# Two 32-column pieces in place of one 64-column piece, for the experts with 96 rows

## The chip, the cores and the metric

The kernel runs on one core of one Trainium2 chip. The metric is the device time of a run in microseconds (us), the median of three runs. One further execution was recorded by the hardware profiler; its rows are what the argument rests on. Engines are named as in the profile: PE is the matrix engine (TensorE), PEld its weight loads, DVE, ACT, POOL and SP the vector, scalar, GpSimd and sync engines; SPq is SP's queue, which issues the transfers.

## The reference

A transformer of three layers on 256 tokens and 256 context tokens, in fp32. Each layer has a mixer and then a mixture of experts. The change is in the first layer's mixture, where all 512 tokens pass through 16 experts of 1024 hidden features; every token goes to two of them. Per expert, with `xblk` the tokens that chose it:

```python
def expert_block(args):
    xblk, e = args
    hid = jax.nn.silu(xblk @ w_gate[e]) * (xblk @ w_up[e])
    return hid @ w_down[e]
```

Each of the three matrices of an expert is 1024 x 1024 fp32, 4.19 MB, so an expert has 12.58 MB of weights. The second layer has the same kind of experts on 256 tokens, the third layer 32 smaller ones.

## The kernel before

**Experts and places.** The experts of the first layer run one after another in 16 places, 0 to 15. A place has a fixed number of rows (tokens), from the table `PLAN`: 96 in places 0, 2, 4, 6, 8, 9, 11, 12 and 14 (nine of them), 32 in place 3, and 64 in the other six. In the second layer every place has 64 rows.

**How an expert is tiled.** The tokens are the stationary operand (loaded into the array), the weights stream through as the moving operand, 512 columns at a time. The contraction (1024) is cut into eight steps k of 128. With 64 rows only half of the array's 128 columns are taken, so two products stand side by side: columns 0 to 63 of the array take one half of a weight's 1024 columns, 64 to 127 the other (line 1595, tiles `gu0` for gate and `gu1` for up). Rows 65 to 96 of a 96-row expert are a part of their own: four products stand side by side, 32 columns of the array each, two for gate and two for up (line 1599, tile `gu2`). The function is `expert_wide`; `x64` and `x32` are the two parts, and either can be missing.

The hidden features are then formed on ACT and DVE and transposed by PE (line 1610, lines 1605 to 1612 in all). The last matrix is used in the same two shapes: line 1627 for the 64-row part (tile `py`, 512 moving columns), line 1631 for the 32-row part (tile `py2`, 256 moving columns). At the end `put` writes the weighted results, and `scatter` (line 1563) adds them to the tokens; `gather` (lines 1486 to 1503) collects the tokens of experts that come later. Pieces of gather and scatter are handed to PE between an expert's steps by `s.work()`. They take the whole array, 128 columns.

**An fp32 product on PE.** In the trace each fp32 product of a line is two records, that is two passes over the moving operand, each with its own weight load: line 1599 has 320 products in the program and 640 MATMUL records.

**What sets the order.** The program is not written as one list: a scheduler sorts each engine's instructions by when their operands are due. So the products of an expert don't stand in the same order in each place. In places 0, 2, 11 and 12 they stand as written, for each k gate, up and then the four of the 32-row part. In places 4, 6, 8, 9 and 14 they are sorted by the page of weights that they read, two steps of k at a time.

**Weights.** A page is 1 MB and holds two steps of k of one matrix; an expert has eight pages for gate and up and four for down. In this layer there are 12 pages (four, six and two in three pools), used in turn by `wpage`, so the next expert's page is written into the page that has the same part in the present one, once PE is done with it. SP issues these transfers in order, lines 1579 and 1622.

Of the kernel before, what the change touches and what calls it, by code (L numbers as in the profile page):

```python
# [20 lines left out]
P = 128  # L21
# [26 lines left out]
# rows for the experts of the first layer, in the order in which they run  # L48
PLAN = (96, 64, 96, 32) + (96, 64, 96, 64) + (96, 96, 64, 96) + (96, 64, 96, 64)
# and of the last one; the first experts there have fixed places  # L50
# [8 lines left out]
def _consts():  # L59
# [4 lines left out]
    # rotation: out[m] = sum_p R[p, m] x[p]  # L64
# [33 lines left out]
    # the places of the experts by rank, the larger ones first  # L98
# [15 lines left out]
def apx(t, off, dims):  # L114
    """A view of a tile's free space: `dims` are [stride, count] in elements."""
    a = t.ap
    return AP(t.tensor, t.offset + off, [list(a[0])] + [list(d) for d in dims])


class Halves:  # L120
    """Tiles as one, split in the second axis."""
# [9 lines left out]
class Tokens:  # L131
    """Tiles [128, 2, D] as one [128, 4, D]."""
# [11 lines left out]
class Columns:  # L144
    """The same room as [128, 8, 512]: features x tokens."""
# [13 lines left out]
class K:  # L159
# [24 lines left out]
    def page(self, src, q=None):  # L184
        """Weights [128, 8, n] of DRAM on one or two pages."""
        n = src.shape[2]
        m = 8 if n <= 256 else 4
        ws = []
        for i in range(0, KT, m):
            w = self.t(self.pg, [P, m, n], "pg")  # L190
            (q or self.nc.sync).dma_start(out=w, in_=src[:, i:i + m, :])
            ws.append(w)
        return Halves(ws)

    # ---------------------------------------------------------------- set-up
    def setup(self, ctx, pages):
# [8 lines left out]
        # the tokens, those of the context apart: they are done with early  # L205
# [10 lines left out]
    def vectors(self, ps, vr):  # L216
        """Packed vectors as columns; silu of the conditioning vectors as stationary operands."""
# [15 lines left out]
    # ---------------------------------------------------------------- adaptive modulation  # L233
    def ada_chunk(self, ps, which, j, parts):
        """512 columns of silu(c) @ w: rows 32 g and 32 g + 1 hold the sums over the k groups."""
# [18 lines left out]
    def ada(self, ps, parts, which, vecs):  # L254
        """Vectors of the modulation as columns: ac[:, vector, k, who]."""
# [16 lines left out]
    def gain(self, which, v, gcol):  # L272
        """(1 + scale) * gain in place."""
# [4 lines left out]
    def as_row(self, ps, tag, which, v, who, row):  # L278
        """A vector of the modulation as a row for every token: [128, 1024]."""
# [9 lines left out]
    # ---------------------------------------------------------------- norms  # L289
    def rstd(self, src, n, pool):  # L290
        """1 / sqrt(mean(src^2) + eps) of each row."""
# [14 lines left out]
    def h_transposed(self, ps, pool, hT, tiles, acol, bcol, src=None):  # L306
        """hT[:, k, tokens] = (x * rstd)^T * acol + bcol, as two parts; tiles: (x tile, which vector)."""
# [12 lines left out]
    def transposed(self, ps, pool, hT, g0, who, xn, acol, bcol):  # L320
        """hT[:, k, tokens of tiles g0, g0 + 1] = xn^T * acol + bcol, as two parts."""
# [21 lines left out]
    # ---------------------------------------------------------------- products in three passes  # L343
    def split(self, pool, w, tag, bufs, copy=None):
        """The pages of a weight as two parts, the second on further pages."""
# [15 lines left out]
    def proj_tok(self, ps, hT, t, w, c0, n):  # L361
        """[128 tokens of tile t, n columns] = h @ w[:, c0:c0 + n]"""
# [7 lines left out]
    def proj_feat(self, ps, hT, w, c0, t0, nt):  # L370
        """[128 columns from c0, nt tokens from t0] = (h @ w)^T"""
# [7 lines left out]
    def lower_bounds(self):  # L379
        """lb and 1 - lb as columns [128, dir * 4 + head] of the first layer."""  # L380
# [18 lines left out]
    def head_norm(self, ps, A, o, gate, col, yT, slot):  # L399
        """rms norm over the features of a head [128 tokens, 4 tiles, 128], gate, and yT[:, slot]."""  # L400
# [100 lines left out]
    def rope_t(self, ps, A, src, out):  # L501
        """Axial rotary embedding of 256 tokens on features x tokens, in place in out."""
# [70 lines left out]
    def out_proj(self, ps, A, yT, w, tiles, rows, layer, tmp=None, x0=None):  # L573
        """x += gate * (y @ w), and the router's logits of each tile; w: the two halves of the columns."""
# [12 lines left out]
    def begin_B(self, name):  # L587
        """A pool for what is done with before the mixer's last product."""
# [4 lines left out]
    def end_B(self, st, n, name, h=True):  # L593
        """In its room the normed tokens, as two parts, if asked for, and n pages for the experts' first weights,
        and above them a pool for the last product."""
# [9 lines left out]
    def split_y(self, A, yT, tags):  # L605
        """The mixer's result as two parts."""
# [7 lines left out]
    def router_start(self, ps, A, layer):  # L614
        """The router on x: its weights take the gain, its bias the shift."""
# [33 lines left out]
    def router(self, ps, A, layer, t):  # L649
        """Logits of a tile of tokens, and the tokens' 1 / rms."""  # L650
# [26 lines left out]
    def mixer0(self):  # L677
        tc, nc, I = self.tc, self.nc, self.I
        with ExitStack() as st:
# [29 lines left out]
            # the result takes the room of x, which is read again for the sum  # L709
# [40 lines left out]
    # ---------------------------------------------------------------- second mixer  # L750
# [58 lines left out]
    def swa_block(self, ps, A, q, k, v, b, sink, nsink, swa, yT):  # L809
        """Two heads (of neighbouring key heads) on 128 partitions."""  # L810
# [42 lines left out]
    # ---------------------------------------------------------------- third mixer  # L853
    def early2(self, tmp):
        """What the third mixer needs of the positions and of the decay alone."""
# [39 lines left out]
        # softplus(-lambda) = max(-lambda, 0) + ln(1 + exp(-|lambda|))  # L895
# [15 lines left out]
    def rope_tok(self, A, x, c, s, out):  # L911
        """Rotary embedding of x [128, n, 64], halves apart."""
# [10 lines left out]
    def mixer2(self):  # L923
        tc, nc, I = self.tc, self.nc, self.I
        self.nw2, self.nw4 = 5, 3
        with ExitStack() as st:
# [22 lines left out]
            # the norm of the second block's input and its first layer's in one: x * g * (mean((x g)^2) + eps * ms)^-1/2  # L949
# [190 lines left out]
    def lru(self, ps, A, B, hT, gl, wg, posb, mT):  # L1140
# [13 lines left out]
        for b0 in (0, 2):  # L1154
# [11 lines left out]
            for i in range(2):  # L1166
                # sigmoid(x + b) = (1 + tanh((x + b) / 2)) / 2
# [48 lines left out]
    def ffn_gain(self, which):  # L1216
        """Column of the gain before the experts, and (1 + scale) * gain."""
        self.gain(which, 4, self.vc[:, (V_NF0, V_NF1, V_N2)[which]:][:, 0:8])

    # ---------------------------------------------------------------- experts  # L1220
# [9 lines left out]
    def first_max(self, R, c, weights, tag):  # L1230
        """One-hot of the first largest of the last axis of c [128, nt, n]."""
# [11 lines left out]
    def ranks(self, R, c, m):  # L1243
        """The place of each element of c [128, n, m] in its last axis by falling value, equal ones in order."""
# [12 lines left out]
    def chosen(self, R, rk, goh, E, ng):  # L1257
        """One-hots [128, 2, nt, E] of the first two places rk within the group that goh [128, nt, ng] marks."""
# [41 lines left out]
    def route_softmax(self, R, L, nt, normed):  # L1300
# [8 lines left out]
        def weights():  # L1309
# [9 lines left out]
            # weights p_group * (1, e) / (1 + e) with e = exp(second - first)  # L1319
# [13 lines left out]
    def pad(plan):  # L1333
        """Rows in front of the first expert's, so that the last expert's end a block."""
        return -sum(plan) % P

    def slots(self, ps, R, oh, nt, E, plan):
        """Rows of the experts' buffers for each token's two experts, far off where an expert's cap is passed.
        Also what the rest needs: the row and cap of each expert, counts and places."""
# [16 lines left out]
        if plan == PLAN2:  # L1356
            # experts with more than 32 rows in front, after those whose places are fixed
# [15 lines left out]
        elif len(set(plan)) > 1:  # L1373
            assert plan == PLAN
            # experts by falling count, the first one fixed
# [7 lines left out]
            # the larger buffers for the experts in front  # L1383
# [23 lines left out]
    def pick(self, R, oh, g, tag):  # L1407
        """[128, 2, nt]: the element of g [128, nt, E] that each one-hot marks."""
# [7 lines left out]
    def places(self, s, R, pos, E):  # L1416
        """The expert at each place, as integers."""
# [14 lines left out]
    def beyond(self, R, oh, info, nt, E, plan, ob):  # L1432
        """Rows over the experts' caps, in blocks of ob: each token's rows, the ends of the experts' blocks, their number."""
# [31 lines left out]
    def gather(self, s, G, sl, base, n, xT):  # L1465
        """xT[:, k, 0:n] = the normed tokens of rows base .. base + n of the experts' buffers, features x rows,
        a piece at a time."""
# [499 lines left out]
```

## Time and profile before

| | us |
|---|---|
| median of three runs | 2270.8 |
| lowest, highest | 2268.87, 2275.35 |
| span of the profiled execution | 2265.9 |
| the first layer's experts in it, from the first product of place 0 (481) to the end of place 15 (1106) | 625 |
| PE busy in these | 608.9 |
| the second layer's experts (1420 to 1827) | 407 |

The profiled execution has no time of its own beside its span; the span runs from its first to its last instruction, and the median of the runs is 4.9 us above it. A busy time of PE counts every stretch in which some matmul is under way, also one in which only part of the array works or in which one matmul drains before the next can start. In the timeline's rows, a row is a run of like instructions: its start, its length to the end of the last one, and their count. Since the last one's end lies beyond the point where the next row may start, what a row costs is read from its start to the next row's start.

### The profile page before, as it was taken

How to read it: one execution, taken by the hardware profiler on the slowest of the kernel's cores; microseconds unless marked ns; L12 is line 12 of the kernel's file. 1: busy time of each engine (PE TensorE's matmuls, PEld its weight loads, DVE VectorE, ACT ScalarE, POOL GpSimd, SP SyncE). 2: the span in 40 equal slices, each digit the busy share in tenths (PEclk: the TensorE clock that was granted, in tenths of full speed). 3: DMA queues.
4: the chain of work that ended last, by engine and by line, in shares of the span. 5: the costliest groups of instructions: out<-in, count | busy, mean ns of one | idle time of the engine just before them, and what ended most of it. 6: DMA issues, size and time to landing. Idle time of an engine off the chain costs nothing. (4 is left out here: it accounts for less than half of the span.)

```text
span 2265.9 us, 27806 instructions
## 1 busy us (share of the span) xinstructions
PE 2027.7 (89%) x10931; PEld 987.7 (44%) x10931; DVE 940.5 (42%) x2121; ACT 549.7 (24%) x1010; POOL 246.9 (11%) x203
## 2 busy tenths in 40 slices
PE   6999989979999999999699989998878779879976
PEld 3766666744232322322265464332222245655422
DVE  4537656255432423332445643222111155555513
ACT  4334444132111111111234432010000045421100
POOL 0000000110301101121300000100000011013202
PEclk9999999989999999999899989999999989989988
DMA  8423425338889888889444568999999986779997
GB/s 304 149 75 130 173 93 195 147 138 318 323 324 338 320 301 306 314 315 353 176 167 149 186 260 339 410 409 409 409 409 409 409 284 238 259 258 362 363 369 275
DMA packets 238428, 632.49 MB, mean 279 GB/s; under 512 B 15440, under 2 KB 83024, under 8 KB 234960
## 3 DMA queue, kind: packets, MB, share of 16 engines
q1 hardware_dynamic: 236736, 626.21, 75.0%
q10 hardware_dynamic: 1552, 4.39, 0.5%
q8 instruction: 90, 1.47, 0.3%
q14 instruction: 50, 0.41, 0.1%
HBM read 629.51 MB, written 1.05 MB: 278 GB/s over the span
## 5 line engine op out<-in xcount | busy, mean ns | idle before, releaser
L1595 PE MATMUL gu<-pg,xT 128*64 128x512 f32 x1984 | 475.7, 603 | 26.3 <-DMA pg<-in_moe_w_up_dram 13.9
L1627 PE MATMUL py<-pg,hT 128*64 128x512 f32 x992 | 249.6, 604 | 24.3 <-DVE hT L1612 18.6
L1567 POOL TENSOR_TENSOR xs<-xs,t 128x512 f32<-128x512 f32 x110 | 142.2, 1301 | 1181.5 <-DVE t L1222 1181.4
L1595 PEld LDWEIGHTS gu<-pg,xT 128*64 128x64 f32 x1984 | 125.6, 136 | 313.3 <-issue 243.9
L1546 DVE SCALAR_TENSOR_TENSOR w<-py,swc,w 32x256 fp32r<-32x256 f32 (+3 forms) x142 | 95.5, 673 | 294.5 <-ACT w L1545 291.9
L375 PE MATMUL mm<-hT,wh 128*128 128x512 f32 (+1 forms) x672 | 190.5, 367 | 9.1 <-ACT w L431 5.1
L1545 ACT ACTIVATE w<-py,swc 32x256 fp32r<-32x256 f32 (+3 forms) x142 | 88.2, 621 | 428.0 <-PE py L1627 327.0
L1222 DVE TENSOR_TENSOR hid<-hid,gu 128x512 f32<-128x512 f32 (+2 forms) x52 | 32.8, 631 | 362.2 <-PE gu L1595 297.1
L1222 DVE TENSOR_TENSOR t<-x,w 128x512 f32<-128x512 f32 x156 | 105.8, 689 | 151.1 <-PE x L1563 135.6
L375 PEld LDWEIGHTS mm<-hT,wh 128*128 128x128 f32 x672 | 118.5, 192 | 41.0 <-issue 8.9
L1563 PE MATMUL x<-w,S 128*128 128x512 f32 x312 | 115.8, 450 | 21.2 <-DVE t L1222 9.6
L1658 PE MATMUL gu<-pg,xT 128*32 128x256 f32 (+1 forms) x1024 | 110.6, 436 | 21.8 <-DMA pg<-in_w_up_dram 17.1
L1627 PEld LDWEIGHTS py<-pg,hT 128*64 128x64 f32 x992 | 62.5, 136 | 147.4 <-issue 100.0
L375 PE MATMUL mm<-hT,pg 128*128 128x512 f32 (+1 forms) x336 | 122.5, 366 | 0.6 <-DVE pg L356 0.6
L1605 ACT ACTIVATE hid<-gu 128x512 f32<-128x512 f32 (+1 forms) x41 | 24.4, 595 | 399.8 <-PE gu L1595 373.4
L1495 PE MATMUL x<-oh,h 128*128 128x256 f32 (+2 forms) x704 | 112.2, 293 | 6.3 <-DVE t L1222 2.4
L1495 PEld LDWEIGHTS x<-oh,h 128*128 128x128 f32 x704 | 91.7, 189 | 57.0 <-issue 32.4
L1599 PE MATMUL gu<-pg,xT 128*32 128x512 f32 x640 | 108.1, 604 | 0.0
L1498 ACT ACTIVATE xT<-x,ac 128x256 f32<-128x256 f32 (+2 forms) x88 | 48.3, 549 | 214.8 <-PE x L1495 214.6
L1563 PEld LDWEIGHTS x<-w,S 128*128 128x128 f32 x312 | 50.7, 193 | 108.3 <-issue 31.8
L356 DVE TENSOR_TENSOR pg<-pg,wh 128x1024 fp32r<-128x1024 f32 (+1 forms) x74 | 89.1, 1211 | 20.1 <-ACT wh L355 20.0
L366 PE MATMUL mm<-wh,hT 128*128 128x512 f32 (+2 forms) x320 | 95.1, 377 | 2.1 <-ACT part L247 0.7
(500 smaller groups left out, 2551.6 us busy)
## 6 DMA issues: line engine op xcount, KB each, us to landing
pg<-in_moe_w_gate_dram SPq DMA_DIRECT2D x128, 1024.0 KB, 8.0
pg<-in_moe_w_up_dram SPq DMA_DIRECT2D x128, 1024.0 KB, 8.9
pg<-in_moe_w_down_dram SPq DMA_DIRECT2D x128, 1024.0 KB, 8.6
pg<-in_ada_w_dram SPq DMA_DIRECT2D x48, 1024.0 KB, 6.2
pg<-in_w_gate_dram SPq DMA_DIRECT2D x32, 1024.0 KB, 11.6
pg<-in_w_up_dram SPq DMA_DIRECT2D x32, 1024.0 KB, 11.7
pg<-in_w_down_dram SPq DMA_DIRECT2D x32, 1024.0 KB, 11.2
pg<-in_w_ada_dram SPq DMA_DIRECT2D x24, 1024.0 KB, 6.9
```

What stands on the lines that cost most here:

```text
L356: nc.vector.tensor_tensor(out=u[:, k:k + m], in0=x[:, k:k + m], in1=t[:, k:k + m].bitcast(F32), op=ALU.subtract)
L366: self.nc.tensor.matmul(out=pm, lhsT=hT[i][:, k, t * P:(t + 1) * P], rhs=w[j][:, k, c0:c0 + n], start=(m == 0), stop=(m == len(ops) - 1))
L375: self.nc.tensor.matmul(out=pm, lhsT=w[i][:, k, c0:c0 + P], rhs=hT[j][:, k, t0:t0 + nt], start=(m == 0), stop=(m == len(ops) - 1))
L1222: self.nc.vector.tensor_tensor(out=out, in0=a, in1=b, op=op)
L1495: nc.tensor.matmul(out=px[:, w, :], lhsT=l_, rhs=r_, start=(i == 0), stop=(i == len(ops) - 1))
L1546: nc.vector.scalar_tensor_tensor(out=lo[o:o + m, c0:c0 + w], in0=x, scalar=wc[o:o + m, :], in1=h.bitcast(F32), op0=ALU.mult, op1=ALU.subtract)
L1563: nc.tensor.matmul(out=px, lhsT=S[0:m, t * P:(t + 1) * P], rhs=y[0:m, cols], start=(i == 0), stop=(i == len(parts) - 1))
L1567: (nc.vector if last and h else nc.gpsimd).tensor_tensor(out=o, in0=o, in1=x, op=ALU.add)
L1595: nc.tensor.matmul(out=o[64 * g:64 * g + 64, :], lhsT=x64[0][:, k, x64[1]:x64[1] + 64], rhs=w[:, 512 * g:512 * g + 512], **f)
L1599: nc.tensor.matmul(out=pq[32 * q:32 * q + 32, :], lhsT=x32[0][:, k, x32[1]:x32[1] + 32], rhs=wk[q // 2][:, 512 * (q % 2):512 * (q % 2) + 5 ...
L1627: nc.tensor.matmul(out=py[64 * h:64 * h + 64, :], lhsT=h64[:, b, 64 * g:64 * g + 64], rhs=w[:, kk, 512 * h:512 * h + 512], **f)
L1658: nc.tensor.matmul(out=pg[r * e:r * e + r, 256 * i:256 * i + 256], lhsT=xT[:, k, c0 + r * e:c0 + r * e + r], rhs=ws[e][:, k, :], start=(k ...
```

## The change

In `expert_wide` the width of a piece of the 64-row part becomes a variable, `m64`: 64 as before where there is no 32-row part, and 32 where there is one. A 64-row part then runs as four products side by side instead of two, 32 columns of the array each: two pieces of 32 rows for each half of the weight's columns. The sums are the same, in the same places of PSUM. The new file also has no comments, so its lines are others: 1595 became 1598, 1599 became 1602, 1610 became 1613, 1627 became 1631 and 1631 became 1635.

```diff
+        m64 = 32 if x32 else 64
...
                 for w, o in zip(wk, (pg, pu)) if x64 else ():
-                    for g in range(2):
-                        nc.tensor.matmul(out=o[64 * g:64 * g + 64, :], lhsT=x64[0][:, k, x64[1]:x64[1] + 64],
+                    for q in range(0, P, m64):
+                        g, r = divmod(q, 64)
+                        nc.tensor.matmul(out=o[q:q + m64, :], lhsT=x64[0][:, k, x64[1] + r:x64[1] + r + m64],
                                          rhs=w[:, 512 * g:512 * g + 512], **f)
...
-                for h in range(2) if x64 else ():
-                    nc.tensor.matmul(out=py[64 * h:64 * h + 64, :], lhsT=h64[:, b, 64 * g:64 * g + 64],
+                for q in range(0, P, m64) if x64 else ():
+                    h, r = divmod(q, 64)
+                    nc.tensor.matmul(out=py[q:q + m64, :], lhsT=h64[:, b, 64 * g + r:64 * g + r + m64],
                                      rhs=w[:, kk, 512 * h:512 * h + 512], **f)
```

The order of PE's instructions at two places of the program follows. A row is a line, the operation, what it writes and reads, the stationary columns by the moving columns, and a count of products. SP's order, and so that of the transfers, is the same in both kernels.

PE in place 11, the first two steps of k, as they were (`pg_1320` is a page of gate, `pg_1321` one of up):

```order
L1595 MATMUL gu0_1317_6286<-pg_1320_6289,xT_1123_5309 64x512 x2
L1595 MATMUL gu1_1318_6287<-pg_1321_6290,xT_1123_5309 64x512 x2
L1599 MATMUL gu2_1319_6288<-pg_1320_6289,xT_1123_5309 32x512 x2
L1599 MATMUL gu2_1319_6288<-pg_1321_6290,xT_1123_5309 32x512 x2
L1595 MATMUL gu0_1317_6286<-pg_1320_6289,xT_1123_5309 64x512 x2
L1595 MATMUL gu1_1318_6287<-pg_1321_6290,xT_1123_5309 64x512 x2
L1599 MATMUL gu2_1319_6288<-pg_1320_6289,xT_1123_5309 32x512 x2
L1599 MATMUL gu2_1319_6288<-pg_1321_6290,xT_1123_5309 32x512 x2
```

and as they are now:

```order
L1598 MATMUL gu0_1317_6574<-pg_1320_6577,xT_1123_5501 32x512 x4
L1598 MATMUL gu1_1318_6575<-pg_1321_6578,xT_1123_5501 32x512 x4
L1602 MATMUL gu2_1319_6576<-pg_1320_6577,xT_1123_5501 32x512 x2
L1602 MATMUL gu2_1319_6576<-pg_1321_6578,xT_1123_5501 32x512 x2
L1598 MATMUL gu0_1317_6574<-pg_1320_6577,xT_1123_5501 32x512 x4
L1598 MATMUL gu1_1318_6575<-pg_1321_6578,xT_1123_5501 32x512 x4
L1602 MATMUL gu2_1319_6576<-pg_1320_6577,xT_1123_5501 32x512 x2
L1602 MATMUL gu2_1319_6576<-pg_1321_6578,xT_1123_5501 32x512 x2
```

Nothing changes its turn; the 64-column pairs have become 32-column fours, so the width is 32 throughout where it went between 64 and 32.

PE in place 4, the first two steps of k, as they were (`pg_1006` gate, `pg_1007` up):

```order
L1595 MATMUL gu0_1003_4661<-pg_1006_4664,xT_871_4018 64x512 x2
L1599 MATMUL gu2_1005_4663<-pg_1006_4664,xT_871_4018 32x512 x2
L1595 MATMUL gu0_1003_4661<-pg_1006_4664,xT_871_4018 64x512 x2
L1595 MATMUL gu1_1004_4662<-pg_1007_4665,xT_871_4018 64x512 x2
L1599 MATMUL gu2_1005_4663<-pg_1007_4665,xT_871_4018 32x512 x2
L1595 MATMUL gu1_1004_4662<-pg_1007_4665,xT_871_4018 64x512 x2
L1599 MATMUL gu2_1005_4663<-pg_1006_4664,xT_871_4018 32x512 x2
L1599 MATMUL gu2_1005_4663<-pg_1007_4665,xT_871_4018 32x512 x2
```

and as they are now:

```order
L1598 MATMUL gu0_1003_4757<-pg_1006_4760,xT_871_4066 32x512 x4
L1602 MATMUL gu2_1005_4759<-pg_1006_4760,xT_871_4066 32x512 x2
L1598 MATMUL gu0_1003_4757<-pg_1006_4760,xT_871_4066 32x512 x4
L1598 MATMUL gu1_1004_4758<-pg_1007_4761,xT_871_4066 32x512 x4
L1602 MATMUL gu2_1005_4759<-pg_1007_4761,xT_871_4066 32x512 x2
L1598 MATMUL gu1_1004_4758<-pg_1007_4761,xT_871_4066 32x512 x4
L1602 MATMUL gu2_1005_4759<-pg_1006_4760,xT_871_4066 32x512 x2
L1602 MATMUL gu2_1005_4759<-pg_1007_4761,xT_871_4066 32x512 x2
```

Here too each stands at its old turn. The two products of `gu2` that stand alone take two of the four groups of 32 columns: the gate's the first two, the up's the last two.

## Rows read from the trace of the kernel before

**Rows 1.** Page: the span.

```profile
span 2265.9 us, 27806 instructions
```

**Rows 2.** Windows: stretch, length, busy PE, PEld, DVE, ACT, POOL; clock, DMA, GB/s.

```profile
481.00:1106.00 625.00, 608.91 (x3345) 195.65 (x3343) 224.61 (x429) 93.88 (x165) 93.80 (x72) 1.00 0.85 313
1106.00:1420.00 314.00, 283.35 (x1415) 166.02 (x1416) 159.80 (x417) 111.84 (x219) 11.96 (x12) 0.92 0.58 212
1420.00:1827.00 407.00, 343.93 (x1508) 110.36 (x1506) 79.43 (x138) 31.29 (x49) 36.24 (x28) 1.00 1.03 409
```

**Rows 3.** Waits of PE, 481 to 1106: us in total, times, longest.

```profile
PE py L1627 <- DVE hT L1612: 7.4, 9, 1.2
PE x L1563 <- DVE t L1222: 1.9, 5, 0.4
```

**Rows 4.** Waits of SP's queue, 481 to 1106.

```profile
SPq L1622 <- PE gu L1599: 135.2, 20, 32.4
```

**Rows 5.** Timeline of PE: start, length, operation; places 5 and 11.

```profile
698.69 5.37 PE L1595 MATMUL gu<-pg,xT 128*64 128x512 f32 x24
...
925.74 1.94 PE L1595 MATMUL gu<-pg,xT 128*64 128x512 f32 x8
927.60 1.07 PE L1599 MATMUL gu<-pg,xT 128*32 128x512 f32 x8
928.60 1.94 PE L1595 MATMUL gu<-pg,xT 128*64 128x512 f32 x8
...
953.34 1.08 PE L1627 MATMUL py<-pg,hT 128*64 128x512 f32 x4
954.35 0.64 PE L1631 MATMUL py<-pg,hT 128*32 128x256 f32 x8
954.92 1.08 PE L1627 MATMUL py<-pg,hT 128*64 128x512 f32 x4
```

**Rows 6.** Timeline of PE, place 4: two steps of k.

```profile
645.62 1.08 PE L1595 MATMUL gu<-pg,xT 128*64 128x512 f32 x4
646.62 1.05 PE L1599 MATMUL gu<-pg,xT 128*32 128x512 f32 x4
647.61 1.94 PE L1595 MATMUL gu<-pg,xT 128*64 128x512 f32 x8
649.47 1.05 PE L1599 MATMUL gu<-pg,xT 128*32 128x512 f32 x4
650.46 1.08 PE L1595 MATMUL gu<-pg,xT 128*64 128x512 f32 x4
651.47 1.07 PE L1599 MATMUL gu<-pg,xT 128*32 128x512 f32 x8
652.46 1.08 PE L1595 MATMUL gu<-pg,xT 128*64 128x512 f32 x4
```

**Rows 7.** Timeline of PE and of its weight loads, place 3 (32 rows).

```profile
606.98 2.74 PE L1599 MATMUL gu<-pg,xT 128*32 128x512 f32 x18
609.65 0.50 PE L1563 MATMUL x<-w,S 128*128 128x512 f32 x1
...
607.41 0.13 PEld L1599 LDWEIGHTS gu<-pg,xT 128*32 128x32 f32 x4 [0.30 <-issue]
607.84 0.13 PEld L1599 LDWEIGHTS gu<-pg,xT 128*32 128x32 f32 x4 [0.30 <-issue]
```

**Rows 8.** Groups by line, 481 to 1106: busy, mean ns, idle before.

```profile
L1599 PEld LDWEIGHTS gu<-pg,xT 128*32 128x32 f32 x640 | 16.2, 108 | 79.2 <-issue 78.1 <-ACT w L1545 0.8
```

**Rows 9.** Windows of places 3, 4, 11 and 13, as in rows 2.

```profile
607.00:639.00 32.00, 29.71 (x220) 15.14 (x214) 22.79 (x43) 9.67 (x19) 10.44 (x8) 1.00 1.01 391
639.00:682.00 43.00, 42.22 (x234) 9.08 (x232) 7.23 (x21) 3.84 (x8) 0.00 (x0) 1.00 0.82 299
...
923.00:961.00 38.00, 37.22 (x234) 8.79 (x230) 6.69 (x11) 4.12 (x7) 0.00 (x0) 1.00 0.89 331
...
1005.00:1032.00 27.00, 27.00 (x118) 9.62 (x116) 12.96 (x20) 3.23 (x7) 10.49 (x8) 1.00 1.02 401
```

## The prediction

> **What bounds the kernel now.** I began with the page's span of 2265.9 us [rows 1] and the windows by stage. The change touches only places of the first layer's mixture that have a 32-row part, so its stage is 481 to 1106. There PE is busy 608.91 of 625 us at full granted clock, and the transfers bring 313 GB/s [rows 2]. The waits of PE come next: the largest is 7.4 us in nine waits for the transposed hidden features, the second 1.9 us, and none of them is a wait for a transfer [rows 3]. The transfers' own queue waits for PE to give pages back, 135.2 us in its largest entry [rows 4]. So in this stage PE is what ends last, and what PE saves ends the stage earlier. The second layer's experts, at 409 GB/s [rows 2], are the other kind of stage: they have no 32-row part and their code is as it was.
>
> A busy PE is not yet a full PE, so I read its timeline for what a step costs.
>
> Length of a pass. Eight more records in a run of 64-wide pairs are four more rounds (a round: one pass in all column groups). From x8 with 1.94 us to x24 with 5.37 us are eight rounds in 3.43 us [rows 5]: 0.429 us a round. In the 32-wide run of place 3, 18 records are nine products in four groups: the first group has three products of two passes, so six rounds lie between 606.98 and 609.65, 2.67 us [rows 7], 0.429 each and 0.1 for the end. The two widths have the same round. Below, a unit is two rounds, 0.859 us, in which all groups finish one 512-column product.
>
> Price of a change of width. A block of 64-wide records with x8 starts at 925.74, and the 32-wide one behind it at 927.60: 1.86 us for four rounds (1.72). The 32-wide one with x8 takes to 928.60: 1.00 for two rounds (0.86). In the last product, 1.01 for 0.86 and 0.57 for two rounds of 256 columns, 0.43 [rows 5]. Each block costs 0.14 to 0.15 us over its rounds; I take 0.145. Within one width the outputs go from gate to up and back without such a cost: the x24 run does it.
>
> Half-filled blocks. In place 4, in two steps of k, two blocks are 32-wide with x4, two products in two of the four groups; each takes 0.99 us to the next row, as does the full one with x8 [rows 6]. Two steps take 645.62 to 652.46, 6.84 us: seven units (6.01) and six blocks (0.87). Only six units of work are in them.
>
> **The change, part by part.** It adds 48 products to each 96-row expert (32 in gate and up, 16 in down) and no other work; a unit has the same length, so the work of a column group stays 24 units in gate and up plus 12 in down (8 and 4 halved), 36 an expert.
>
> (1) Widths. From the order of the products I count where the width changes in a place, the whole-array pieces included. Before: 40, 39, 43, 43, 43, 54, 34, 40 and 43 in places 0, 2, 4, 6, 8, 9, 11, 12 and 14, in all 379. After: 16, 13, 4, 5, 5, 18, 5, 12 and 5, in all 83. What remains are the changes to and from gather, scatter and transposes. 296 fewer at 0.145 are 42.9 us; pieces of gather that moved add four in places 1, 3 and 5, 0.6. That is 42.3.
>
> (2) Half-filled blocks. In places 4, 6, 8 and 14 the two products that stood alone between 64-wide blocks now stand between 32-wide ones. A group that they leave free can go on with the next products: the first pair delays groups 0 and 1, the second groups 2 and 3, and after six units all groups are level. One unit less in two steps, four an expert: 4 x 4 x 0.859 = 13.7 us. In place 9 pieces of scatter stand between the two pairs and keep seven units; there (1) alone counts. In place 4 the whole check reads: 41 units (35.2) and 43 blocks (6.2) make 41.4, and the window has 43 [rows 9], so 1.6 are the transposes and the wait for them. After: 37 units (31.8) and 4 blocks (0.6), with the same rest 34.
>
> No row shows two column groups of different tiles at different products. Bounds: if a group waits until all are free, (2) gives 0; if it doesn't, 13.7. In the 32-wide run of place 3 the ninth product starts in group 0 as its turn comes, with no block between k steps [rows 7]; it is the nearest row, and I take 13.7. For (1) the bounds are 0.145 and, if a 32-wide stream that goes between tiles kept some cost, 0; the x24 run, which goes between tiles and keeps none, is nearest.
>
> (3) What may come back. The 0.8 us waits for the transposed features stay, nine of them. The last 32-row block covered the DVE step ahead of the transposes; it becomes 0.14 shorter, nine times, 1.3 us if nothing else covers. Groups that are half a product apart at an expert's end cost up to 0.4 in five places, and scatter behind place 5's kind of start keeps its 1.9 us of waits. I take 2 us.
>
> (4) Transfers. A page is asked for when the expert before gives the same page back [rows 4], a whole expert ahead. After, a 96-row expert of the dense kind takes about 34 us, and 12.58 MB in 34 us is 370 GB/s; places 3 and 13 were served at 391 and 401 [rows 9]. So they stay hidden, with a margin of 6 to 8%. If the cover went, an expert at 331 GB/s, what place 11 has now [rows 9], would take 38 us.
>
> (5) Weight loads. Four of 108 ns instead of two a round [rows 8]. In place 3 four loads begin together, end in 0.13 us and recur every 0.43 us [rows 7], under the passes. Cost 0. If each round paid its 0.13, 9 x 72 rounds would cost 84 us.
>
> Beside this, the Trainium skill, page "TensorE: Matmul & The Clock Gate", section "Part 3: Packing small matmuls — row/col tiling", says that weight loads run under matmuls in flight only where the row group differs. All products here use all 128 rows, so by that rule no load would be hidden, and the sum would be the 84 us loss of the last sentence set against the gain. The trace does not agree: the loads of rows 7 come 0.43 us apart, the length of a bare round.
>
> Sum: 42.3 + 13.7 - 2 = 54 us. On the profiled span that is 2265.9 - 54 = 2212; the median of the runs is 4.9 above the span, so 2270.8 - 54 = 2217 us. The later stages I let move as a whole: the mixer that follows draws 212 GB/s, far under the 409 of the mixture behind it [rows 2], so an earlier start finds the transfers free, and the pages of that mixture are given back by the mixer, which starts earlier by as much.
>
> **The rivals.**
> Main case, both terms: 2217, own range 2210 to 2224. Chance 0.70.
> Groups wait for each other: (2) falls, 42.3 - 2 = 40, 2231. For it: no row shows mixed tiles. Against: place 3's odd runs. 0.13.
> Transfers end last: places 4, 6, 8, 11 and 14 stop at 38 us instead of 34 (place 11: 33), 21 us given back, 33 us gain, 2238. For it: the margin is thin, and the stage's mean must rise from 313 to 343 GB/s (195.6 MB in 571 us). Against: 391 to 409 in rows 2 and 9. 0.06.
> The block's cost isn't the width's, but stands wherever the 32-row part alternates with the other: (1) falls, 13.7 - 2 = 12, 2259. Against: it appears at every change between 64, 32 and the whole array, and nowhere else. 0.03.
> Slower: the loads of a long 32-wide stream are not hidden. Place 3's runs are short; a stream of 24 units an expert could use up what was loaded ahead. At 0.13 a round the net is 84 - 54 = 30, so 2301; it decides from 54 / 648 rounds = 0.083 us a round. Against: six rounds in a row show nothing. 0.03.
> The change does not take effect in time: transfers capped at the stage's present mean of 313 GB/s, PE waiting as long as it saves, 2271. Against: the queue waits for PE, not the reverse [rows 4]. 0.03.
> The last 0.02 I leave to what I do not see, faster or not.
>
> **How the numbers follow.** About 0.3% (7 us) tells a change from none here. Faster by more: 0.70 + 0.13 + 0.06 + 0.03 and half of the rest, 0.93. Within: 0.03 and a little, 0.04. Slower: 0.03. The range takes in the main case with its own uncertainty and the two next ones with theirs: 2207 to 2238. It leaves out about 0.11.
>
> **What would show it.** In the timeline after, a 96-row expert has one unbroken 32-wide run in gate and up where no piece of gather or scatter stands; its rounds recur every 0.43 us. Step (1): place 11 takes about 33 us for 38. Step (2): two steps of k in place 4 take 5.2 us for 6.84; 6.0 would be the first rival. Step (3): PE's waits in the stage near 16 us, as now. Step (4): no wait of PE for a page of gate, up or down there; the stage's rate near 343 GB/s. Step (5): loads 0.13 us long in fours. The stage should end near 1052 for 1106, and what follows should keep its length. The prediction is wrong if rounds grow beyond 0.43, if PE waits for pages, or if the stages behind give time back.

## The result, and the profile after

| | before | after |
|---|---|---|
| median, us (four runs each) | 2270.1 | 2213.6 |
| lowest, highest | 2268.9, 2275.4 | 2210.0, 2221.6 |
| ratio of the times, 95% interval | 1 | 0.9747 (0.9731 to 0.9763) |
| span of the profiled execution | 2265.9 | 2219.7 |
| first layer's experts, in it | 624.99 | 566.68 |

The change saves 56.5 us on the medians, where 54 was forecast (2217 us against 2213.6). The interval of the ratio allows 53.8 to 61.1 us.

The two profiles differ by 46 us of span only, so the stages have to be set against each other one by one. First the windows from the first product of place 0 to the end of place 15, the mixer behind, and the rest of the program. Of the kernel before (columns as in [rows 2]):

```profile
481.19:1106.18 624.99, 608.73 (x3344) 195.56 (x3343) 224.44 (x430) 94.01 (x165) 93.80 (x72) 1.00 0.85 313
1106.18:1362.53 256.35, 225.88 (x1142) 143.13 (x1142) 140.69 (x354) 100.82 (x200) 11.96 (x12) 0.91 0.51 179
1362.53:2265.90 903.37, 769.25 (x4170) 343.62 (x4169) 312.09 (x706) 165.63 (x319) 113.42 (x91) 0.96 0.94 352
```

and of the changed one, with a short stretch near its end:

```profile
488.12:1054.80 566.68, 551.39 (x4208) 224.32 (x4207) 224.95 (x430) 94.19 (x165) 94.02 (x72) 1.00 0.91 345
1054.80:1311.19 256.39, 225.16 (x1142) 142.51 (x1142) 140.60 (x354) 100.80 (x200) 11.95 (x12) 0.91 0.51 179
1311.19:2219.70 908.51, 772.41 (x4170) 346.08 (x4169) 312.02 (x706) 165.75 (x319) 114.40 (x91) 0.96 0.94 350
...
1893.00:1906.00 13.00, 12.75 (x58) 7.53 (x62) 6.28 (x14) 5.11 (x9) 0.76 (x2) 0.50 0.31 104
```

The stage of the change is 58.3 us shorter; PE is busy 57.3 us less in it and idle 1.0 us less (16.3 before, 15.3 after). PE's records are 864 more, and its weight loads are busy 29 us more, all under other work. The transfers' rate rises from 313 to 345 GB/s. The mixer behind it has its old length to 0.04 us. The 12 us by which the spans fall short of the 58 are 7 us ahead of the stage (it starts at 488 for 481, and the change touches nothing ahead of it) and 5 us behind it. The last row shows 13 us at the lower of TensorE's two levels (a granted clock of 0.50, 1.2 GHz); the same place of the program before, 51.3 us later, had the full one:

```profile
1944.30:1957.30 13.00, 12.62 (x93) 8.53 (x94) 10.44 (x20) 9.98 (x17) 0.56 (x1) 1.00 0.68 237
```

Such a stretch comes and goes by the run: of the ten profiles of this study, from the first expert of the second layer to PE's last record, five take 894.4 to 895.3 us (the kernel before among them), one 897.0 and four 899.6 to 900.0 (the changed kernel among them). Exactly those four have 13.7 us at a granted clock of 0.50 at this place. In the 6.9 us ahead of it PE was busy for 6.90 us; at the same place of the kernel before, where the clock stayed at its full level, for 6.70. So these rows do not show why it fell. The changed kernel's profiled run is the longest of its four, 2221.6 us. For that reason the stage is compared below, not the span.

Place 11 in PE's timeline after, which answers to the middle of [rows 5]:

```profile
888.86 1.92 PE L1598 MATMUL gu<-pg,xT 128*32 128x512 f32 x16
890.60 1.04 PE L1602 MATMUL gu<-pg,xT 128*32 128x512 f32 x8
891.46 1.90 PE L1598 MATMUL gu<-pg,xT 128*32 128x512 f32 x16
893.18 1.04 PE L1602 MATMUL gu<-pg,xT 128*32 128x512 f32 x8
...
908.63 1.04 PE L1602 MATMUL gu<-pg,xT 128*32 128x512 f32 x8
909.69 0.66 PE L1613 MATMUL tp<-cst,hid 128*128 128x128 f32 x4
```

From 890.60 to 893.18 is one step of k, three units: 2.58 us, 0.86 each. Nothing is left of the 0.14 to 0.15 us that each block cost. Its weight loads, in the same stretch (the last bracket is what ended the engine's idle time):

```profile
893.18 0.13 PEld L1602 LDWEIGHTS gu<-pg,xT 128*32 128x32 f32 x4 [0.30 <-issue]
893.61 0.13 PEld L1598 LDWEIGHTS gu<-pg,xT 128*32 128x32 f32 x4 [0.30 <-issue]
894.04 0.13 PEld L1598 LDWEIGHTS gu<-pg,xT 128*32 128x32 f32 x4 [0.30 <-issue]
```

Four loads in 0.13 us every 0.43 us, as in [rows 7]: hidden in the long run too. The sentence of the Trainium skill on loads that was set against the change ("TensorE: Matmul & The Clock Gate", "Part 3: Packing small matmuls — row/col tiling") does not hold here as it stands: every product uses all 128 rows, and the loads still lie under the passes. The same section also lets a load go ahead into a background weight buffer; whether that is what happens here, no row shows.

Place 4 after, two steps of k, which answers to [rows 6]:

```profile
637.80 1.04 PE L1598 MATMUL gu<-pg,xT 128*32 128x512 f32 x8
638.66 0.60 PE L1602 MATMUL gu<-pg,xT 128*32 128x512 f32 x2
638.67 0.62 PE L1598 MATMUL gu<-pg,xT 128*32 128x512 f32 x2
639.09 0.60 PE L1602 MATMUL gu<-pg,xT 128*32 128x512 f32 x2
639.12 1.85 PE L1598 MATMUL gu<-pg,xT 128*32 128x512 f32 x12
640.41 0.60 PE L1602 MATMUL gu<-pg,xT 128*32 128x512 f32 x2
...
642.09 1.06 PE L1602 MATMUL gu<-pg,xT 128*32 128x512 f32 x8
642.95 1.06 PE L1598 MATMUL gu<-pg,xT 128*32 128x512 f32 x8
```

The rows of line 1602 and of line 1598 start 0.01 to 0.04 us apart: two column groups run the 32-row part while the other two already run the next product. Two steps go from 637.80 to 642.95, 5.15 us for 6.84, which is six bare units (5.15).

PE's waits in the stage after, which answer to [rows 3] (us in total, times, longest):

```profile
PE py L1631 <- DVE hT L1615: 6.2, 8, 0.8
PE x L1563 <- DVE t L1222: 2.8, 5, 0.9
PE x L1563 <- ACT w L1545: 1.8, 3, 0.8
PE tp L1613 <- DVE hid L1222: 1.7, 2, 0.9
```

No wait for a transfer is among them. The windows of places 4, 11 and 9 after, in this order; the first two answer to [rows 9]:

```profile
637.80:671.87 34.07, 33.28 (x333) 12.46 (x325) 7.43 (x21) 3.37 (x7) 0.00 (x0) 1.00 0.94 359
888.86:922.00 33.14, 32.34 (x325) 11.58 (x327) 6.66 (x11) 3.91 (x6) 0.00 (x0) 1.00 0.96 364
807.31:850.93 43.62, 43.53 (x357) 14.51 (x349) 16.71 (x27) 6.08 (x11) 10.66 (x8) 1.00 0.82 307
```

and of place 9 before:

```profile
835.96:885.33 49.37, 48.00 (x250) 11.30 (x249) 16.39 (x27) 5.43 (x11) 10.57 (x8) 1.00 0.69 249
```

Place 4 takes 34 us and place 11 33 us, as forecast; place 9 is 5.75 us shorter. The window of place 9 begins 0.8 us before the last products of place 8 are done, since its first products go into a column group that is already free; places 8 and 9 together went from 92.86 to 76.77 us.

### The profile page after: what moved, and what is told of

It is laid out like the page before. It is cut to its first block, busy times and chain, and to the rows that moved or that the text cites. A ratio compares the mean times of both kernels' runs of the same rounds, so it can differ in the third digit from the quotient of the medians.

```text
span 2219.7 us, 29536 instructions
## 1 busy us (share of the span) xinstructions
PE 1978.9 (89%) x11795; PEld 1023.2 (46%) x11795; DVE 940.9 (42%) x2121; ACT 549.9 (25%) x1010; POOL 248.2 (11%) x203
## 5 line engine op out<-in xcount | busy, mean ns | idle before, releaser
L1598 PE MATMUL gu<-pg,xT 128*64 128x512 f32 (+1 forms) x2560 | 489.0, 598 | 27.1 <-DMA pg<-in_moe_w_up_dram 14.6
L1631 PE MATMUL py<-pg,hT 128*64 128x512 f32 (+1 forms) x1280 | 258.5, 597 | 23.6 <-DVE hT L1615 17.4
L1598 PEld LDWEIGHTS gu<-pg,xT 128*64 128x64 f32 (+1 forms) x2560 | 132.5, 124 | 297.9 <-issue 227.7
L1631 PEld LDWEIGHTS py<-pg,hT 128*64 128x64 f32 (+1 forms) x1280 | 77.0, 124 | 137.4 <-issue 76.2
L1563 PE MATMUL x<-w,S 128*128 128x512 f32 x312 | 112.9, 442 | 22.8 <-DVE t L1222 11.5
```

Of the source, the lines that this page charges most:

```text
L1563: nc.tensor.matmul(out=px, lhsT=S[0:m, t * P:(t + 1) * P], rhs=y[0:m, cols], start=(i == 0), stop=(i == len(parts) - 1))
L1598: nc.tensor.matmul(out=o[q:q + m64, :], lhsT=x64[0][:, k, x64[1] + r:x64[1] + r + m64], rhs=w[:, 512 * g:512 * g + 512], **f)
L1631: nc.tensor.matmul(out=py[q:q + m64, :], lhsT=h64[:, b, 64 * g + r:64 * g + r + m64], rhs=w[:, kk, 512 * h:512 * h + 512], **f)
```

## The experiments

The theory is the prediction's: a price for each change of the array's width, and a unit saved for each two half-filled blocks. Its rivals: all of the gain is the width's, or it belongs to the turn between the two parts of an expert, or a 32-wide product is cheaper in itself. Blocks and units below are counted from the order of the products, from place 0 to the end of place 15, all kernels alike: 491 blocks and 514 units before, 199 and 498 after. Each stage length, and each busy time of PE in it, is from one profile. The runs were made in three groups, each with runs of the kernel before beside it (medians 2270.1, 2271.7 and 2272.8 us), and each ratio is to those.

| kernel | blocks, units | median, us | ratio to before, 95% interval | stage, us | PE busy in it |
|---|---|---|---|---|---|
| before | 491, 514 | 2270.1 to 2272.8 | 1 | 624.99 | 608.73 |
| after | 199, 498 | 2213.6 | 0.9747 (0.9731 to 0.9763) | 566.68 | 551.39 |
| gate_up_alone | 330, 498 | 2232.9 | 0.9830 (0.9813 to 0.9846) | 587.60 | 572.95 |
| down_alone | 356, 514 | 2250.9 | 0.9902 (0.9885 to 0.9918) | 602.36 | 587.38 |
| mixed_64 | 274, 498 | 2225.6 | 0.9793 (0.9777 to 0.9809) | 577.53 | 562.91 |
| all_32 | 191, 499 | 2214.0 | 0.9747 (0.9730 to 0.9763) | 565.21 | 550.94 |
| pairs | 177, 499 | 2214.2 | 0.9751 (0.9734 to 0.9768) | 566.29 | 549.84 |
| split_copy | 201, 496 | 2217.0 | 0.9754 (0.9741 to 0.9768) | 567.23 | 553.25 |
| split_pairs | 179, 497 | 2213.4 | 0.9741 (0.9726 to 0.9756) | 564.77 | 550.33 |
| little_32 | not counted | 2158.3 (one run) | none | 506.33 | 472.00 |

**Half of the change: gate and up.** Against the changed kernel:

```diff
-                for q in range(0, P, m64) if x64 else ():
+                for q in range(0, P, 64) if x64 else ():
...
-                    nc.tensor.matmul(out=py[q:q + m64, :], lhsT=h64[:, b, 64 * g + r:64 * g + r + m64],
+                    nc.tensor.matmul(out=py[q:q + 64, :], lhsT=h64[:, b, 64 * g + r:64 * g + r + 64],
```

> The 64-row part of the 96-row experts runs 32 wide in gate and up, 64 wide in down. From the order: 330 blocks of one width from place 0 to the end of place 15 (491 before, 199 after the change), and 498 units of work (514 before, 498 after), so the half-filled blocks of places 4, 6, 8 and 14 are gone as in the changed kernel. Theory (a price of 0.145 us for each block, and a unit of 0.859 us saved for each half-filled pair of blocks): 161 blocks fewer than before are 23.3 us, 16 units 13.7, together 37: 2270 - 37 = 2233 us; against the changed kernel (2214) +19. Place 4 takes 37 units, 21 blocks and the rest of 1.6 us: 36.4 us (42.8 before, 34.1 after). Rival, all of the gain of 56.5 is in the changes of width, 0.19 us each, and none in the half-filled blocks: 161 x 0.19 = 31 us, 2239, place 4 at 42.8 - 22 x 0.19 = 38.6. Rival, a 32-wide product costs less in itself: two thirds of the products that changed are here, 38 us, 2232.

Measured: 2232.9 us, and place 4 takes 36.26 us. Both are the theory's (2233, 36.4); the rival without the half-filled blocks wanted 2239 and 38.6. The rival of a cheaper 32-wide product wanted 2232 (and by the same reckoning 2251 for the other half, below), which these times can't tell from the theory; it is decided by the two runs on the 64-row experts that follow.

**The other half: down.** The same edit in the loop of gate and up:

```diff
-                    for q in range(0, P, m64):
+                    for q in range(0, P, 64):
...
-                        nc.tensor.matmul(out=o[q:q + m64, :], lhsT=x64[0][:, k, x64[1] + r:x64[1] + r + m64],
+                        nc.tensor.matmul(out=o[q:q + 64, :], lhsT=x64[0][:, k, x64[1] + r:x64[1] + r + 64],
```

> The other half of the change: the 64-row part of the 96-row experts runs 32 wide in down, 64 wide in gate and up. 356 blocks and 514 units: changes of width go, half-filled blocks stay. Theory: 135 blocks fewer than before at 0.145 us are 19.6 us, 2270 - 19.6 = 2250 us; place 4 takes 41 units, 27 blocks and 1.6 us: 40.7 us. Rival, all in the changes of width at 0.19 us: 25.6 us, 2244, place 4 at 39.8. Rival, the cost of the block is not the width's: no gain, 2270.

Measured: 2250.9 us, place 4 at 40.64 us (theory 2250 and 40.7; with all of the gain in the changes, at 0.19 us each, 2244 and 39.8). Its timeline in place 4 has the half-filled blocks still:

```profile
645.50 1.08 PE L1598 MATMUL gu<-pg,xT 128*64 128x512 f32 x4
646.51 1.05 PE L1602 MATMUL gu<-pg,xT 128*32 128x512 f32 x4
647.49 1.94 PE L1598 MATMUL gu<-pg,xT 128*64 128x512 f32 x8
649.36 1.05 PE L1602 MATMUL gu<-pg,xT 128*32 128x512 f32 x4
...
651.35 1.06 PE L1602 MATMUL gu<-pg,xT 128*32 128x512 f32 x8
652.35 1.08 PE L1598 MATMUL gu<-pg,xT 128*64 128x512 f32 x4
```

645.50 to 652.35 is 6.85 us for the two steps, the 6.84 of [rows 6]; the 32-wide blocks with x4 take 0.98 us. So it is the width of gate and up that fills them. The two halves save 37.4 and 22.6 us of the stage, together 60.0 where the whole saves 58.3.

**Changes of width put back elsewhere.** In the 64-row experts every second step of k runs 32 wide; the same is done in down.

```diff
-                    for q in range(0, P, m64):
+                    mw = 32 if s.layer == 0 and kk else m64
+                    for q in range(0, P, mw):
...
-                        nc.tensor.matmul(out=o[q:q + m64, :], lhsT=x64[0][:, k, x64[1] + r:x64[1] + r + m64],
+                        nc.tensor.matmul(out=o[q:q + mw, :], lhsT=x64[0][:, k, x64[1] + r:x64[1] + r + mw],
```

> The changed kernel, and in the six experts of the first layer that have 64 rows and no 32-row part (places 1, 5, 7, 10, 13, 15) every second step of k runs 32 wide, in gate, up and down: same work, more changes of width, and nothing else. 274 blocks for 199 of the changed kernel, units the same. Theory: 75 more changes at 0.145 us cost 10.9 us, 2214 + 11 = 2225; the places grow by 8, 16, 17, 12, 10 and 17 blocks (less one taken away each in places 11 and 13's neighbours), so place 7 from 36.0 to about 38.5 us. Rival, the block's cost is not the width's but stands where a 64-row and a 32-row part alternate: 0, 2214. Rival, 32-wide products cost less in themselves: 144 of them against 432 in the change, a third of 56 us, so 19 us faster, 2195.

Measured: 2225.6 us; the stage is 10.85 us longer than the changed kernel's, 0.145 us for each of the 75 changes (11.5 us by PE's busy time, 0.154). Of these, 0.8 us are in place 14, where no width differs from the changed kernel (34.91 us for 34.09); without it the price is 0.134, or 0.143 by the busy time. At 0.19 us a change, the price that would put the whole gain into the widths, it would be 14 us. There is no 32-row part in these places, so the rival that the cost lies in the turn between the parts falls, and so does the cheaper 32-wide product. The place that grows most is place 7, from 36.02 to 38.21 us.

**No change of width in the 64-row experts.**

```diff
-        m64 = 32 if x32 else 64
+        m64 = 32 if x32 or s.layer == 0 else 64
```

> The changed kernel, and the six 64-row experts of the first layer run 32 wide throughout as well: nothing is 64 wide in that stage. 191 blocks (199), 499 units (498). Theory: 8 changes fewer, 1.2 us, one unit more, 0.9 us: as the changed kernel, 2214 with 2 us to either side. Rival, 32-wide products cost less in themselves: 288 of them against 432, two thirds of 56 us, 2177. Rival, a weight load that is not quite hidden in a long 32-wide stream: 0.13 us in each of 6 x 48 rounds, 37 us, 2251.

Measured: 2214.0 us, as the changed kernel. A 32-wide product is neither cheaper nor dearer in itself, and long streams of it hide their loads. Beside the run before it, this one also shows one change of width by itself. In place 5, a page of gate or up (two steps of k) between the same whole-array pieces; in mixed_64 one step is 64 wide and the next 32:

```profile
685.38 2.07 PE L1599 MATMUL gu<-pg,xT 128*64 128x512 f32 x12
687.38 0.96 PE L1563 MATMUL x<-w,S 128*128 128x512 f32 x3
```

and in all_32 both are 32 wide:

```profile
681.10 1.92 PE L1598 MATMUL gu<-pg,xT 128*32 128x512 f32 x16
682.95 1.20 PE L1563 MATMUL x<-w,S 128*128 128x512 f32 x4
```

From start to start 2.00 us against 1.85: 0.15 us for one change, with the same work and the same neighbours. The Trainium skill, page "TensorEngine Tiling (Array Packing)", section "Key Properties", says that a change of tiling mode drains the engine, and that tiles within a mode run independently; these rows give the first its price here, and the rows of place 4 above, with two lines at work at once, agree with the second.

**Fewer whole-array pieces between.** The side work is handed out by twos; the same edit stands in down:

```diff
-            s.work()
+            if k2 % 4 == 2:
+                s.work()
+                s.work()
```

> The changed kernel, where the side work of the experts (gather, scatter and put) is handed out two pieces at a time behind every second page and no longer one piece behind each, so that fewer whole-array pieces break the 32-wide run. 177 blocks for 199, 499 units for 498. Theory: 22 x 0.145 - 0.9 = 2.3 us faster than the changed kernel, 2214 - 2 = 2212 us. Rival, two pieces in a row wait for the PSUM buffer or the DVE step of the first: up to 0.9 us in each of some 20 pairs, 2225 to 2232.

Measured: 2214.2 us, the same as the changed kernel. PE's busy time fell by 1.55 us, near the 2.3 expected, but PE's idle time grew from 15.3 to 16.5 us: the rival's wait, in small.

**The copy of the hidden features in two halves.** Down then reads `h64[b // 2][:, b % 2, ...]`, and `h32` in the same way.

```diff
-            ht = self.t(M, [P, 4, n], f"hT{n}", bufs=1)
-            nc.vector.tensor_copy(ht, tp)
+            ht = [self.t(M, [P, 2, n], f"hT{n}{i}", bufs=1) for i in range(2)]
+            for i in range(2):
+                nc.vector.tensor_copy(ht[i], tp[:, 2 * i:2 * i + 2, :])
```

> The changed kernel, where the copy of the transposed hidden features out of PSUM (hT, 0.69 us on DVE) is made as two copies of half the size into two tiles, so that the first products of down wait for the first half alone. PE's wait for it stands in the trace of the changed kernel with 6.2 us in eight waits. Theory (the wait is a price of its own, on PE's path, not covered by the width of the block ahead): 0.3 us less in each of eight, 2.4 us, and two units less by the order, 1.7: 2214 - 4 = 2210 us. Rival, PE then waits for the second half or DVE's two copies cost more than one: 2214, same.

Measured: 2217.0 us, the same within its interval. The wait did shorten (hT 3.6 us in seven, for 6.2 in eight), but the order of the pieces moved with it, and PE's busy time grew by 1.9 us; the 4 us did not come. Most of that growth stands in one row, down's products of place 5, the same 32 records in one 64-wide run. In the changed kernel, and then in this one:

```profile
697.05 7.09 PE L1631 MATMUL py<-pg,hT 128*64 128x512 f32 x32 [0.79 <-DVE hT L1615]
...
691.75 8.78 PE L1632 MATMUL py<-pg,hT 128*64 128x512 f32 x32 [0.52 <-DVE hT L1616]
```

The windows of this kernel ahead of it and in it:

```profile
688.30:692.00 3.70, 1.97 (x12) 0.76 (x10) 1.42 (x3) 0.00 (x0) 0.00 (x0) 1.00 1.04 406
692.00:695.40 3.40, 3.40 (x10) 0.98 (x8) 0.02 (x1) 0.00 (x0) 0.00 (x0) 0.50 0.89 323
```

For 3.4 us the granted clock was at the lower level (0.50, 1.2 GHz), after 3.7 us in which PE was busy for 1.97; that costs this profile 1.69 us, and the changed kernel's has no such stretch in its stage. The rest of the growth is 0.2 us; by the count the busy time should have fallen by 1.4, and that remainder is not explained.

**Both edits.** The diffs of the last two together.

> Both edits of the two runs before this one. 179 blocks for 199, 497 units for 498. Theory: 2.9 + 0.9 + 2.4 = 6 us faster than the changed kernel, 2208 us. Rival, as there: 2214 to 2230.

Measured: 2213.4 us with an interval of 0.9726 to 0.9756, which can't be told from the changed kernel's 0.9747. None of these three versions is clearly faster than the changed kernel; what they change of the widths and of this wait is within the noise.

**Less work for PE, the same transfers.** Left out are seven of eight steps of k of the 32-row part in the 96-row experts; the same edit stands in down.

```diff
-                if x32:
+                if x32 and (k == 0 or s.layer or not x64):
+                    if x64 and s.layer == 0:
+                        f = dict(start=True, stop=True)
```

> The changed kernel with seven of the eight products of k of the 32-row part left out in the nine 96-row experts, in gate, up and down (the output lacks that part): PE has 9 x 10.5 units = 94.5 x 0.859 = 81 us less to do there, the transfers are the same 195.6 MB. It shows how much room the transfers of the stage have. Theory of the prediction (transfers stay hidden at 343 GB/s and can reach about the 409 of the second layer's experts): PE alone would end the stage 81 us earlier, at 490 us, 399 GB/s on the mean; a dense 96-row place would take 24 us of PE but 31 us for its 12.58 MB at 409, so PE waits for pages now and some 20 us come back: about 2153 us, the stage at 510 us and 384 GB/s. Rival, the transfers are at their limit after the change already: no gain, 2214, 343 GB/s. Rival, they have room beyond 409: 2133.

Measured: 2158.3 us in one run, the stage 506.3 us at 386 GB/s: near the theory's 2153, 510 and 384, but for another reason than it gave. PE's busy time fell by 79.4 us (81 expected; 3.4 us of place 3 ran at a granted clock of 0.50, after 3.5 us in which PE was busy for 1.59, which is an estimated 1.7 us of the difference), and its idle time rose from 15.3 to 34.3. The 19 us are not waits for pages. PE's waits in that stage:

```profile
PE py L1633 <- DVE hT L1617: 8.7, 11, 0.8
PE tp L1615 <- DVE hid L1222: 8.6, 10, 0.9
PE x L1563 <- ACT w L1545: 6.7, 9, 1.7
PE x L1563 <- DVE t L1222: 6.1, 14, 0.9
```

and the window from the end of place 6 to the end of place 14:

```profile
700.00:960.00 260.00, 242.61 (x1659) 89.12 (x1652) 109.78 (x187) 45.17 (x78) 52.61 (x40) 1.00 1.02 403
```

The 32-row part's products are also the cover for ACT's and DVE's steps ahead of the transposes (hid: 8.6 us for 1.7) and for scatter's. The transfers ran at 403 GB/s over 260 us, the 409 of [rows 2] nearly, and the pages in hand still sufficed. The changed kernel's 345 is far from that on the mean, though its place 14 alone runs at 409, also without a wait. Whether the transfers have room beyond 409, the last rival, the run does not show.

## Why the prediction held, step by step

**What bounds the stage: right.** PE was busy 97% of it before and is after; what PE saved, the stage saved, and the mixer behind moved as a whole (256.39 us for 256.35).

**Step (1), widths: right.** 42.3 us from 0.145 us a change. Two edits and a pair of rows give the price: 0.145 from mixed_64's stage and 0.154 from its busy time (0.134 and 0.143 without place 14); 0.158 from the busy time of down_alone (21.35 us for 135 changes); 0.15 from the pair of rows. In places 0, 4, 9, 11 and 12 of down_alone, PE's busy time is 1.76 to 2.23 us shorter for 12 or 15 blocks fewer, 0.146 to 0.149 each. Where nothing else changed it came as worked out: places 11 and 12 together went from 81.73 to 73.37 us, 8.4 us for 57 blocks. With 0.147 the 292 changes that the count of the stage has fewer are 43 us, with 0.155 45.

**Step (2), half-filled blocks: right.** This was the step that rested on no row of mixed tiles. Place 4's two steps take the 5.15 us forecast as 5.2 (6.0 was the rival's), and places 4, 6 and 14 are 8.8, 9.4 and 9.4 us shorter, for 9.1 worked out (41 units and 43 blocks less 37 and 4 or 5). That the two terms are separate is shown by the halves: with 64-wide gate and up the blocks stay at 0.98 us. How the sum splits to the microsecond stays open: of the 57.3 us of busy time, 14.4 are left for this term with 0.147 a change and 12 with 0.155, for 13.7.

**Step (3), what comes back: wrong in sign.** I took 2 us of longer waits, and PE's idle time fell by 1.0. The wait for hT has lost one of its nine; in place 9 PE was idle 1.4 us of 49.37 and is 0.1 us of 43.62. DVE's step ahead of the transposes did not become visible (hid 1.7 us in two waits); a scatter piece waits a little more (2.8 for 1.9). Those 3 us, with the 1.3 that busy time fell beyond the 56 of (1) and (2), are the 4 us by which 58.3 exceeds the 54. That the medians differ by 56.5, nearer to the forecast than the stage, is no merit of the sum: the four runs of the changed kernel alone lie between 2210.0 and 2221.6. Place 9 also lost 4.5 us of busy time, by (1) alone, for 5.2 worked out; places 8 and 9 together lost 14.6 (90.50 to 75.90) for 14.2.

**Step (4), transfers: right, with somewhat more room than I gave them.** 345 GB/s for the 343 expected, and no wait of PE for a transfer. The margin of 6 to 8% was read from single places; little_32 held 403 GB/s over 260 us without a wait of PE for a page. That rival (2238) and the cap at 313 (2271) are gone.

**Step (5), weight loads: right.** 0.13 us of every 0.43, hidden, in the longest streams of all_32 too (no loss of the 37 us that a cost of 0.13 a round would bring there). The slower rival (2301) is gone.

**What stays open.** Why some runs have the 13 us at the half clock near the end, and why the profiles start the stage at 480 to 488 us, was not tried; no code differs in either place between these kernels.

## What to carry to other kernels

Count how often PE changes the width of its tiles: each change cost about 0.15 us here, so small parts should share one width even if that doubles the number of instructions, as long as the weight loads stay under the passes. Look in the timeline for blocks whose count is half of the full one at the full length: within one width the free column groups take the next products, across widths they stand idle. And before work is taken off PE, see which ACT and DVE steps it covers: in one profile, 79 us less work for PE gave 60.

## What the runs showed of the hardware that was not expected

Within one width the column groups do not wait for each other across tiles or pages: in place 4 the rows of two lines start 0.01 to 0.04 us apart for whole stretches, and the two steps take exactly their work. The price of a change between 64 and 32 is 0.15 us in the pair of rows; for changes to and from whole-array pieces only pairs speaks, with 1.55 us of busy time and a unit more for 22 changes, 0.11 each, from one profile. And 29 us more of weight loads in the stage cost nothing that a run could show.
